# Two units of the second feed-forward product split ahead of the last Relus, a weight sum formed in SBUF, and a job stream that begins elsewhere

## The chip, the cores and the metric

The kernel runs on one core of one Trainium2 chip. The time is the device time of one execution in microseconds (us), the median of several runs. Its engines work side by side, each with its own instruction queue: TensorE (PE in the profile; PEld is its weight load), VectorE (DVE), ScalarE (ACT), GpSimd (POOL) and SyncE (SP). An instruction waits at the head of its queue until what it needs is there, and everything behind it waits too. DMAs are issued by SP and POOL here, each in its queue's order.

## The reference, cut to what matters

One layer of a streaming encoder, for 512 positions of width 1024, in float32. Three mixers (gated DeltaNet, "GDN"; stick-breaking attention; a short gated convolution) are merged by gates, projected and normed, and a feed-forward network with squared Relu follows. The part that the change is about:

```python
h2 = rms_norm(x1, norm_ffn_pre)              # x1: 512 x 1024
a = jnp.square(jax.nn.relu(h2 @ w_ff1))      # 512 x 4096
y = a @ w_ff2                                # 512 x 1024
x = x1 + rms_norm(y, norm_ffn_post)
```

## The kernel before

**Precision.** TensorE multiplies fp32r numbers. A float32 matrix is split into a rounded part `hi` and the rest `lo`, and a product is made of three: hi·hi, hi·lo, lo·hi (`mm3`, or `go` in `product`). ScalarE makes `hi` by a copy, VectorE makes `lo` by a subtraction (`split`; `wload` for weights).

**The order of the work.** The first part interleaves GDN, stick-breaking and projections by hand-written generators that `tick()` advances. `gate_branch` is the unit of the gate stage: a projection, a sigmoid into `sg`, the load of half a unit of branch weights (`wload`, 256 KB), twelve matmuls and a multiplication. It runs for branches 1 and 2 with GDN and stick-breaking work in between (the loop that makes `mp`), then for branch 0 together with the loads of the output weights `wo` (`load_wo`). The last of these makes `mg`, the merged activations, and the out-projection (`out_k`, into PSUM banks `po`) follows, with norms whose vectors `wpo` and `wff` and whose rows `x1` come over POOL's queue. Instructions are put in order by priorities; a step inside `with early():` gets a priority ahead of the place where it stands in the code, so weight loads and their splits run ahead as far as buffers allow. `g2` tiles are a shared pool of 128x512 buffers.

**First product (FF1).** 32 steps `f`, each 128 of the 4096 channels: load of 512 KB into `raw`, its split into `hl` (a ring of three), 24 matmuls, then `ff1_act`: ScalarE's Relu (L945), VectorE's squares into `aT` (L948), and for the later half the differences `X` (L951) and `W` (L953).

**Second product (FF2).** It is a two-by-two block product done with seven products in place of eight (in order Q, R, Q, R, S, V, S by the PSUM banks they go to), each of eight units `u` of 12 matmuls. Per unit, `stat` splits the left side (activations `aT`, or `X`, `W`) into `ahi` and `alo`, a ring of four, and `right` loads a 512 KB weight unit and splits it into `hl`. The first three units load into six `rw` tiles; all later ones into eight slots `ch` that share memory with FF1's input (`h2h`, `h2l`) and so come free when FF1 ends.

**The jobs.** Four of the seven products need sums or differences of weight blocks: S5, S6, S1, S7, eight tiles each in DRAM. `presum()` does one step of this stream: SP copies one block from DRAM to DRAM (the base, `dma_start` in L173), and two steps later POOL adds the other block to it by an accumulating DMA (L169). There are 32 jobs, of 512 KB each; a step is taken in FF1 for f = 3 to 27, and in the products after every fourth unit. The last product reads S7.

Of the kernel before, what the change touches and what calls it, by code (L numbers as in the profile page):

```python
# [9 lines left out]
F32 = mybir.dt.float32  # L10
F32R = mybir.dt.float32r
AF = mybir.ActivationFunctionType
ALU = mybir.AluOpType

P = 128
D = 1024
# [45 lines left out]
def trunk_kernel(ctx, tc, keys, xT, xtok, wst, wab, cst, vec, alog, dtb, wpost, wffn, wfpost, out):  # L62
# [22 lines left out]
    def mbank():  # L85
        return pp.tile([P, 512], F32, tag="mm", bufs=3, name=nm("mm"))
# [59 lines left out]
    def wsrc(n, *key):  # L146
        if key not in keys:
# [1 line left out]
        return wst[keys.index(key)][:, :n]  # L149


    S5, S6, S1, S7 = ([dp.tile([P, 1024], F32, tag=f"{n}{u}", bufs=1, name=f"{n}{u}") for u in range(8)]
                      for n in ("S5", "S6", "S1", "S7"))
    jobs = []
    for u in range(8):
        jobs.append((S5[u], ("ff2", 1, 8 + u), ("ff2", 1, u)))
# [1 line left out]
        jobs.append((S6[u], ("ff2", 0, u), ("ff2", 1, u)))  # L158
    for u in range(8):
        jobs.append((S1[u], S5[u], ("ff2", 0, u)))  # L160
    for u in range(8):
        jobs.append((S7[u], S1[u], ("ff2", 0, 8 + u)))
    added = []
    LAG = 2

    def presum():
        while added and (len(added) > LAG or not jobs):
            t, key = added.pop(0)
            nc.gpsimd.dma_start(t, wsrc(1024, *key), accum_op=ALU.add, max_dma_last_dim=4096)  # L169
        if jobs:  # L170
            t, of, plus = jobs.pop(0)
            with early():
                dep(nc.sync.dma_start(t, wsrc(1024, *of) if isinstance(of, tuple) else of), lastw[0])  # L173
            added.append((t, plus))

    def wnext(*key):
        return wload(wsrc(1024, *key))
# [624 lines left out]
    def gate_branch(dm, i, y):  # L802
        sg = g2("sg")
        ps = proj(5128 + i * D + dm * P)
        with urgent():
            act(sg, ps, AF.Sigmoid)
        w = wload(wsrc(512, "br", i, dm), 512)
        ps = mbank()
        for k in range(4):
            c = slice(k * P, k * P + P)  # L810
            mm3(ps, w[:, 0, c], w[:, 1, c], y[k][0], y[k][1], k == 0, k == 3)
            if k in (1, 3):
                tick()
        with urgent():
            nc.vector.tensor_tensor(sg, sg, ps, ALU.mult)
        return sg

    for dm in range(8):
        a = gate_branch(dm, 1, yb)
        b = gate_branch(dm, 2, yc)  # L820
        mp[dm] = g2("mp")
        nc.vector.tensor_tensor(mp[dm], a, b, ALU.add)
# [111 lines left out]

    aT = [[], []]
    X, W = [], []
    flat = lambda t: t.rearrange("p j c -> p (j c)")

    def ff1_act(f, ps):
        u = f // 2  # L940
        if f % 2 == 0:
            for i in range(2):
                aT[i].append(g2("aT", F32, (P, 2, 256)))
        r = sm.tile([P, 512], F32, tag="r", bufs=2, name=nm("r"))
        nc.scalar.activation(r, ps, AF.Relu)  # L945
        for i in range(2):
            c = slice(i * 256, i * 256 + 256)
            nc.vector.tensor_tensor(aT[i][u][:, f % 2, :], r[:, c], ps[:, c], ALU.mult)  # L948
        if f % 2 == 1 and u >= 8:
            X.append(g2("X", F32, (P, 2, 256)))  # L950
            nc.vector.tensor_tensor(flat(X[-1]), flat(aT[0][u]), flat(aT[0][u - 8]), ALU.subtract)  # L951
            W.append(aT[0][u])
            nc.vector.tensor_tensor(flat(W[-1]), flat(W[-1]), flat(aT[1][u]), ALU.subtract)  # L953
# [6 lines left out]
    for f, (w, ps) in enumerate(lead):  # L960
        ff1_mm(w, ps, slice(256, 512))
        ff1_act(f, ps)
    for f in range(3, 32):
        if f < 28:
            presum()
        w = wnext("ff1", f)
        ps = mbank()
        ff1_mm(w, ps, slice(0, 512))
        ff1_act(f, ps)

    wfp = sm.tile([P, D], F32, tag="L", bufs=1, name="wfp")
    nc.gpsimd.dma_start(wfp, wfpost.partition_broadcast(P))
    NU2 = 8
    A = {(i, k): aT[i][8 * k:8 * k + 8] for i in range(2) for k in range(2)}  # L980
    ou, x1a = {}, {}
    NJ, NR = 4, 3
    stats = [(g2("ahi", F32R, (P, 2, 256)), g2("alo", F32R, (P, 2, 256))) for _ in range(NJ)]
    raws = [[(slice(0, 512), g2("rw")), (slice(512, 1024), g2("rw"))] for _ in range(NR)]
    turn = {"s": 0, "r": 0, "w": 0}
    slot = [0]

    def ring(what, of):
        turn[what] += 1
        return of[(turn[what] - 1) % len(of)]  # L990

    def right(src):
        if turn["r"] < NR:
            raw = ring("r", raws)
        else:
            if turn["r"] == NR:
                raws.clear()
                for _ in range(2):
                    t = hp.tile([P, 4, 1024], F32, tag="h16", name=nm("ch"))
                    raws.extend([(slice(0, 1024), t[:, i, :])] for i in range(4))  # L1000
            raw = ring("r", raws)
        for c, r in raw:
            x = nc.sync.dma_start(r, src[:, c])
            dep(x, lastw[0])
            lastw[0] = x
        turn["w"] += 1
        if turn["w"] % 4:
            hl = wp.tile([P, 2, 1024], F32R, tag="hl", bufs=3, name=nm("hl"))
            hl = (hl[:, 0, :], hl[:, 1, :])
        else:  # L1010
            hl = [wp.tile([P, 1024], F32R, tag="raw", bufs=2, name=nm("hl4")) for _ in range(2)]
        for c, r in raw:
            nc.scalar.copy(hl[0][:, c], r)  # L1013
            nc.vector.tensor_tensor(hl[1][:, c], r, rf(hl[0][:, c]), ALU.subtract)  # L1014
        return hl

    def block(k, n):
        return lambda u: wsrc(1024, "ff2", n, 8 * k + u)

    def stat(t):  # L1020
        hi, lo = ring("s", stats)
        split(flat(hi), flat(lo), flat(t))
        return hi, lo

    def product(ps, left, block, first, tail=0):
        def go(tb, a, w, f, l):
            ts_ = slice(tb * P, tb * P + P)
            for j in range(2):
                c = slice(j * 512, j * 512 + 512)
                mm(ps[tb], a[0][:, j, ts_], w[0][:, c], f and j == 0, False, not first)  # L1030
                mm(ps[tb], a[0][:, j, ts_], w[1][:, c], False, False, not first)
                mm(ps[tb], a[1][:, j, ts_], w[0][:, c], False, l and j == 1, not first)

        kept = []
        for u in range(NU2):
            with early():
                a = stat(left(u))
                w = right(block(u))
            slot[0] += 1
            if slot[0] % 4 == 0:  # L1040
                presum()
            if u >= NU2 - tail:
                kept.append((a, w, u == NU2 - 1))
                continue
            for tb in range(2):
                go(tb, a, w, first and u == 0, u == NU2 - 1)
        for tb in range(2):
            for a, w, l in kept:
                go(tb, a, w, False, l)
            yield tb  # L1050
# [20 lines left out]

    d, ga = ([g2(n) for _ in range(2)] for n in ("d", "ga"))
    Q = banks2("Q")
    for tb in product(Q, lambda u: A[1, 0][u], block(0, 0), True):
        nc.scalar.copy(d[tb], Q[tb])
    R = banks2("R")
    for tb in product(R, lambda u: X[u], block(1, 1), True):
# [15 lines left out]
    for tb in product(V, lambda u: sub(A[1, 0][u], X[u], X[u]), lambda u: S6[u], True):  # L1093
        nc.vector.tensor_tensor(d[tb], V[tb], d[tb], ALU.add)
        evac(d[tb], 2 + tb, 1)
        store(2 + tb)
    for tb in product(S, lambda u: W[u], lambda u: S7[u], False, 2):
        nc.vector.tensor_tensor(ga[tb], S[tb], ga[tb], ALU.add)
        evac(ga[tb], tb, 0)
        store(tb)  # L1100
# [85 lines left out]
```

## Time and profile before

| What | us |
| --- | --- |
| median of 3 runs | 924.14 (922.2 to 926.25) |
| the profiled execution | 924.36 |
| its span | 922.6 |
| TensorE busy | 889.2 (96%) |
| VectorE busy | 602.8 (65%) |
| ScalarE busy | 440.7 (48%) |
| GpSimd busy | 119.8 (13%) |

The span is cut by the profile into 40 equal slices; a digit of 9 is 90% busy or more. TensorE, its granted clock and the DMA engines:

```profile
PE   8999999989998999999999989999999979999996
PEclk9999999999999999999999999999999999999998
DMA  9322223221211132412243475399999529996522
```

The out-projection lies in slices 24 and 25, FF1 in slices 26 to 33, FF2 in the rest. A busy TensorE is not TensorE at full speed: its matmuls take twice as long where the clock is granted at the lower of its two levels. The rows of the trace that say more stand further down.

### The profile page before, as it was taken

Reading aid. Unit: us, or ns where it says so; the run is one execution under the profiler, and the core shown is the slowest. Engines: PE = TensorE matmul, PEld = TensorE weight load, DVE = VectorE, ACT = ScalarE, POOL = GpSimd, SP = SyncE. Lnnn points to the kernel's source line nnn. Section 1 sums busy time; section 2 is a strip of 40 time slices with the busy share of each in tenths; the row PEclk is TensorE's granted clock in tenths of the full one; section 3 lists DMA queues with packets and bytes.
Section 4 is the critical chain, followed back from the end, with each engine's and each line's share of the span. In section 5 each row is a group of like instructions: output and inputs, shape, how many; then the busy total and the mean of one; then the engine's idle time right before and its main releaser. Section 6 shows DMA issues by size and latency. Waiting matters only on the chain.

```text
span 922.6 us, 11744 instructions
## 1 busy us (share of the span) xinstructions
PE 889.2 (96%) x4204; PEld 737.7 (80%) x4204; DVE 602.8 (65%) x1046; ACT 440.7 (48%) x799; POOL 119.8 (13%) x189
## 2 busy tenths in 40 slices
PE   8999999989998999999999989999999979999996
PEld 6788888777787888888888868988888868888885
DVE  4786689988878659555555436533344447878885
ACT  7456776537776832232343333322322235566561
POOL 1003331121122120200000032011111000120000
PEclk9999999999999999999999999999999999999998
DMA  9322223221211132412243475399999529996522
GB/s 319 109 71 90 72 94 99 92 80 52 83 41 54 50 121 82 132 66 78 72 157 122 174 201 189 112 282 282 285 285 285 179 86 364 339 321 227 191 97 87
DMA packets 41883, 141.17 MB, mean 153 GB/s; under 512 B 5584, under 2 KB 5584, under 8 KB 41312
## 3 DMA queue, kind: packets, MB, share of 16 engines
q1 hardware_dynamic: 34432, 115.69, 34.9%
q0 software_dynamic: 7248, 24.68, 12.7%
q8 instruction: 33, 0.54, 0.2%
q14 instruction: 26, 0.21, 0.1%
q10 hardware_dynamic: 144, 0.04, 0.0%
HBM read 135.67 MB, written 38.27 MB: 189 GB/s over the span
## 4 chain that ended last, share of the span: by engine, by line
PE 81%; DVE 10%; ACT 3%; DMA 2%; issue 2%; POOL 0%; SPq 0%; POOLq 0%; DVEq 0%; ACTq 0%
PE mm L180 52%; PE Q L180 5%; PE R L180 5%; PE S L180 4%; PE po L180 3%; PE psv L180 3%; PE V L180 2%; DVE hl L143 2%; PE p L180 2%; DMA raw<-wst 2%; DVE c L686 2%; DVE w L678 1%; DVE z L688 1%; DVE XX L508 1%; DVE XX L514 1%
## 5 line engine op out<-in xcount | busy, mean ns | idle before, releaser
L180 PE MATMUL mm<-hh,hl 128*128 128x512 f32 x928 | 306.6, 398 | 0.7 <-ACT ct L735 0.7
L143 DVE TENSOR_TENSOR hl<-raw,hl 128x1024 fp32r<-128x1024 f32 x116 | 129.8, 1119 | 144.1 <-ACT hl L142 143.8
L142 ACT CAST hl<-raw 128x1024 fp32r<-128x1024 f32 x116 | 111.8, 964 | 225.6 <-PE mm L180 173.7
L180 PEld LDWEIGHTS mm<-hh,hl 128*128 128x128 f32 x928 | 174.7, 189 | 35.7 <-ACT ct L735 1.0
L180 PE MATMUL mm<-hl,hl 128*128 128x512 f32 x464 | 181.7, 392 | 0.0
L180 PE MATMUL mm<-h2h,hl 128*128 128x512 f32 (+1 forms) x528 | 155.2, 377 | 0.3 <-ACT h2h L188 0.2
L180 PEld LDWEIGHTS mm<-h2h,hl 128*128 128x128 f32 x528 | 97.2, 188 | 19.0 <-ACT h2h L188 0.8
L180 PEld LDWEIGHTS mm<-hl,hl 128*128 128x128 f32 x464 | 87.8, 189 | 16.1
L180 PE MATMUL mm<-h2l,hl 128*128 128x512 f32 (+1 forms) x264 | 99.5, 377 | 0.1
L1014 DVE TENSOR_TENSOR hl<-ch,hl 128x1024 fp32r<-128x1024 f32 x53 | 64.7, 1223 | 6.5 <-ACT hl L1013 6.4
L169 POOL DMA_DIRECT2D S<-wst x32 | 26.2, 820 | 301.8 <-DMA S<-wst 153.7
L180 PEld LDWEIGHTS mm<-h2l,hl 128*128 128x128 f32 x264 | 49.7, 188 | 9.3 <-DVE h2l L189 0.3
L1013 ACT CAST hl<-ch 128x1024 fp32r<-128x1024 f32 x53 | 55.4, 1046 | 0.0
L180 PE MATMUL po<-wo,mg 128*128 128x512 f32 x192 | 46.9, 400 | 3.4 <-ACT mg L188 3.4
L180 PEld LDWEIGHTS po<-wo,mg 128*128 128x128 f32 x192 | 37.0, 193 | 11.8 <-ACT mg L188 3.9
L180 PE MATMUL Q<-hl,ahi 128*128 128x512 f32 x128 | 41.4, 405 | 4.6 <-ACT hl L1013 2.8
L180 PE MATMUL S<-hl,ahi 128*128 128x512 f32 x128 | 39.4, 389 | 0.0
L180 PE MATMUL R<-hl,ahi 128*128 128x512 f32 x128 | 39.4, 389 | 0.0
L188 ACT CAST ahi<-aT 128x512 fp32r<-128x512 f32 x32 | 19.7, 623 | 31.7 <-PE Q L180 15.1
L180 PEld LDWEIGHTS Q<-hl,ahi 128*128 128x128 f32 x128 | 25.2, 197 | 10.7 <-ACT hl L1013 3.2
L948 DVE TENSOR_TENSOR aT<-r,mm 128x256 f32<-128x256 f32 x62 | 23.1, 414 | 11.2 <-ACT r L945 11.2
L652 POOL TENSOR_SCALAR_AFFINE_SELECT w<-w 128x128 f32<-128x128 f32 (+1 forms) x24 | 13.7, 580 | 118.7 <-DVE w L678 99.8
(287 smaller groups left out, 1464.9 us busy)
## 6 DMA issues: line engine op xcount, KB each, us to landing
raw<-wst SPq DMA_DIRECT2D x92, 512.0 KB, 3.3
S<-wst POOLq DMA_DIRECT2D x32, 512.0 KB, 9.0
ch<-S SPq DMA_DIRECT2D x32, 512.0 KB, 3.3
raw<-wst SPq DMA_DIRECT2D x48, 256.0 KB, 3.0
ch<-wst SPq DMA_DIRECT2D x21, 512.0 KB, 8.0
S<-wst SPq DMA_DIRECT2D x16, 512.0 KB, 8.4
S<-S SPq DMA_DIRECT2D x16, 512.0 KB, 9.1
xk<-xT SPq DMA_DIRECT2D x8, 256.0 KB, 5.5
```

What stands on the lines that cost most here:

```text
L142: nc.scalar.copy(hl[:, 0, :], raw)
L143: nc.vector.tensor_tensor(hl[:, 1, :], raw, rf(hl[:, 0, :]), ALU.subtract)
L169: nc.gpsimd.dma_start(t, wsrc(1024, *key), accum_op=ALU.add, max_dma_last_dim=4096)
L180: return nc.tensor.matmul(o, l, r, start=start, stop=stop, skip_group_check=more)
L188: nc.scalar.copy(hi, src)
L508: nc.vector.tensor_tensor(tmp[:, :, :w], X[:, :, j].unsqueeze(2).to_broadcast([P, 8, w]), L[:, j, j + 1:].unsqueeze(1).to_broadcast([P, 8, ...
L514: nc.vector.tensor_tensor(X[:, :, j + 1:], X[:, :, j + 1:], tmp[:, :, :w], ALU.subtract)
L652: nc.gpsimd.affine_select(ap, ap, pattern=[[0, n], [-1, 128]], compare_op=ALU.is_ge, fill=0.0, base=-1, channel_multiplier=1)
L686: nc.vector.tensor_tensor_scan(c[:, c0:c0 + m][:, ::-1], ones[:, 0:1].to_broadcast([P, m]), back, 0.0, ALU.mult, ALU.add)
L948: nc.vector.tensor_tensor(aT[i][u][:, f % 2, :], r[:, c], ps[:, c], ALU.mult)
L1013: nc.scalar.copy(hl[0][:, c], r)
L1014: nc.vector.tensor_tensor(hl[1][:, c], r, rf(hl[0][:, c]), ALU.subtract)
```

## The change

In the order of the code:

- S7 and its eight jobs are gone; 24 jobs are left. `right` takes a second source `plus`, which POOL adds by an accumulating DMA to the SBUF slot that SP has just loaded. The last product loads S1[u] and adds block(1, 0) in this way.
- `presum()` is called in the gate loop of branches 1 and 2, at dm = 1, 3, 5, 7, and in FF1 for f = 6 to 29. It is no longer called in the products.
- The tiles and functions of FF2's sides (`stats`, `raws`, `right`, `block`, `stat`) stand ahead of the FF1 loop. The loop ends at f = 29. For f = 30 and 31 the matmuls, and one unit of Q's operands (`unit`: `stat` and `right`, under `early()`), are written ahead of `ff1_act`; `dep` keeps Relu(30) and Relu(31) behind that unit's last cast on ScalarE, and their squares behind its last subtraction on VectorE. `product` takes these two units from `ready`.

```diff
-    S5, S6, S1, S7 = ([dp.tile([P, 1024], F32, tag=f"{n}{u}", bufs=1, name=f"{n}{u}") for u in range(8)]
-                      for n in ("S5", "S6", "S1", "S7"))
+    S5, S6, S1 = ([dp.tile([P, 1024], F32, tag=f"{n}{u}", bufs=1, name=f"{n}{u}") for u in range(8)]
+                  for n in ("S5", "S6", "S1"))
...
-    for u in range(8):
-        jobs.append((S7[u], S1[u], ("ff2", 0, 8 + u)))
...
     for dm in range(8):
+        if dm % 2 == 1:
+            presum()
         a = gate_branch(dm, 1, yb)
         b = gate_branch(dm, 2, yc)
...
+    ready, after = [], [None, None]
...
-        nc.scalar.activation(r, ps, AF.Relu)
+        x = nc.scalar.activation(r, ps, AF.Relu)
+        if ready:
+            dep(x, after[0])
         for i in range(2):
             c = slice(i * 256, i * 256 + 256)
-            nc.vector.tensor_tensor(aT[i][u][:, f % 2, :], r[:, c], ps[:, c], ALU.mult)
+            x = nc.vector.tensor_tensor(aT[i][u][:, f % 2, :], r[:, c], ps[:, c], ALU.mult)
+            if ready:
+                dep(x, after[1])
...
-    for f in range(3, 32):
-        if f < 28:
-            presum()
...
-    def right(src):
+    def right(src, plus=None):
...
             x = nc.sync.dma_start(r, src[:, c])
             dep(x, lastw[0])
             lastw[0] = x
+            if plus is not None:
+                nc.gpsimd.dma_start(r, plus[:, c], accum_op=ALU.add)
...
         for c, r in raw:
-            nc.scalar.copy(hl[0][:, c], r)
-            nc.vector.tensor_tensor(hl[1][:, c], r, rf(hl[0][:, c]), ALU.subtract)
+            after[0] = nc.scalar.copy(hl[0][:, c], r)
+            after[1] = nc.vector.tensor_tensor(hl[1][:, c], r, rf(hl[0][:, c]), ALU.subtract)
...
+    def unit(left, block, u):
+        with early():
+            src = block(u)
+            return stat(left(u)), right(*src) if isinstance(src, tuple) else right(src)
+
+    A10 = lambda u: aT[1][u]
+    for f in range(3, 30):
+        if f >= 6:
+            presum()
+        w = wnext("ff1", f)
+        ps = mbank()
+        ff1_mm(w, ps, slice(0, 512))
+        ff1_act(f, ps)
+    late = [(wnext("ff1", 30), mbank())]
+    ff1_mm(*late[0], slice(0, 512))
+    late.append((wnext("ff1", 31), mbank()))
+    ready.append(unit(A10, block(0, 0), 0))
+    ff1_act(30, late[0][1])
+    ff1_mm(*late[1], slice(0, 512))
+    ready.append(unit(A10, block(0, 0), 1))
+    ff1_act(31, late[1][1])
...
         for u in range(NU2):
-            with early():
-                a = stat(left(u))
-                w = right(block(u))
-            slot[0] += 1
-            if slot[0] % 4 == 0:
-                presum()
+            a, w = ready.pop(0) if ready else unit(left, block, u)
...
-    for tb in product(S, lambda u: W[u], lambda u: S7[u], False, 2):
+    for tb in product(S, lambda u: W[u], lambda u: (S1[u], block(1, 0)(u)), False, 2):
```

**ScalarE, from the Relu of f=29 on** (`r` is a Relu's output, `ahi` the rounded activations, `hl<-rw` the cast of half a weight unit, `ch` a slot). Before:

```order
L945 ACTIVATE r_6392<-mm_6367 128x512
L945 ACTIVATE r_6431<-mm_6404 128x512
L945 ACTIVATE r_6465<-mm_6440 128x512
L188 CAST ahi_6474<-aT_5324 128x512
L188 CAST ahi_6476<-aT_5382 128x512
L188 CAST ahi_6478<-aT_5454 128x512
L1013 CAST hl_6498<-rw_6482 128x512
L1013 CAST hl_6498<-rw_6483 128x512
L188 CAST ahi_6480<-aT_5527 128x512
L1013 CAST hl_6519<-rw_6484 128x512
L1013 CAST hl_6519<-rw_6485 128x512
L1013 CAST hl_6540<-rw_6486 128x512
```

After the change, to the last Relu:

```order
L946 ACTIVATE r_6399<-mm_6374 128x512
L186 CAST ahi_5384<-aT_5321 128x512
L1000 CAST hl_6446<-rw_5392 128x512
L1000 CAST hl_6446<-rw_5393 128x512
L946 ACTIVATE r_6453<-mm_6411 128x512
L186 CAST ahi_5386<-aT_5379 128x512
L1000 CAST hl_6485<-rw_5394 128x512
L1000 CAST hl_6485<-rw_5395 128x512
L946 ACTIVATE r_6490<-mm_6441 128x512
```

and from there on:

```order
L186 CAST ahi_5388<-aT_5463 128x512
L186 CAST ahi_5384<-aT_5609 128x512
L186 CAST ahi_5390<-aT_5535 128x512
L1000 CAST hl_6533<-rw_5396 128x512
L186 CAST ahi_5386<-aT_5683 128x512
L1000 CAST hl_6533<-rw_5397 128x512
L1000 CAST hl_1170_6555<-ch_6552 128x1024
L186 CAST ahi_5388<-aT_5757 128x512
```

The activation split and the two casts of unit 0 now stand before the second of these Relus, those of unit 1 before the third. Behind the Relus come the splits of units 2, 4 and 3, and the split of unit 5 stands between the two casts of unit 2. The splits of units 4 and 5 reuse the ring tiles of units 0 and 1.

**SP, around the last loads of the gate stage** (`raw` at L139 is a projection's weight unit or a branch's, at L832 half of a unit of `wo`; `S_72` to `S_74` are the first jobs' bases, `x1d` the store of the residual). Before:

```order
L832 DMA raw_4695<-wst 128x512
L139 DMA raw_5193<-wst 128x1024
L832 DMA raw_4701<-wst 128x512
L173 DMA S_72<-wst 16x8192
L139 DMA raw_5388<-wst 128x1024
L173 DMA S_73<-wst 16x8192
L832 DMA raw_4763<-wst 128x512
L139 DMA raw_5423<-wst 128x1024
L832 DMA raw_4769<-wst 128x512
L173 DMA S_74<-wst 16x8192
L890 DMA x1d<-x_921_4841 128x512
```

After the change:

```order
L832 DMA raw_4692<-wst 128x512
L139 DMA raw_5190<-wst 128x1024
L832 DMA raw_4698<-wst 128x512
L139 DMA raw_5398<-wst 128x1024
L832 DMA raw_4760<-wst 128x512
L139 DMA raw_5432<-wst 128x1024
L832 DMA raw_4766<-wst 128x512
L890 DMA x1d<-x_921_4838 128x512
```

The three base copies are gone from this stretch; the first four bases now stand among the loads of the gate loop of branches 1 and 2, and the loads of `raw` keep their order.

**POOL, at the first stick-breaking masks of the gate loop** (`gu` is GDN's, `w` the stick-breaking tiles that the triangle mask is applied to). Before:

```order
L391 TENSOR_TENSOR gu_2636<-cs,gah 128x512
L391 TENSOR_TENSOR gu_2638<-cs,gal 128x512
L652 AFFINE_SELECT w_2711<-w_2711 128x128
L652 AFFINE_SELECT w_2712<-w_2712 128x256
L652 AFFINE_SELECT w_2713<-w_2713 128x128
```

After the change:

```order
L389 TENSOR_TENSOR gu_2628<-cs,gah 128x512
L389 TENSOR_TENSOR gu_2630<-cs,gal 128x512
L167 DMA S_72<-wst 128x1024
L650 AFFINE_SELECT w_2703<-w_2703 128x128
L650 AFFINE_SELECT w_2704<-w_2704 128x256
L650 AFFINE_SELECT w_2705<-w_2705 128x128
```

The first job's accumulate stands between the two `gu` and the masks of the next head. In the kernel before it stood behind GDN's last norms, with two more, right before `wpo`:

```order
L613 TENSOR_TENSOR f_4221<-f_4221,half 128x4
L613 TENSOR_TENSOR f_4236<-f_4236,half 128x4
L169 DMA S_72<-wst 128x1024
L169 DMA S_73<-wst 128x1024
L169 DMA S_74<-wst 128x1024
L849 DMA wpo_4829<-wpost 128x512
```

## Rows read from the trace of the kernel before

**Rows 1.** The page, part 1: busy us (share) and instructions of each engine

```profile
PE 889.2 (96%) x4204; PEld 737.7 (80%) x4204; DVE 602.8 (65%) x1046; ACT 440.7 (48%) x799; POOL 119.8 (13%) x189
```

**Rows 2.** Waits of TensorE, the whole span: who waits, for whom: us, times, longest

```profile
PE po L180 <- ACT mg L188: 3.4, 1, 3.4
PE Q L180 <- ACT hl L1013: 2.8, 1, 2.8
...
PE Q L180 <- DVE hl L1014: 1.8, 1, 1.8
PE p L180 <- DVE ct L582: 1.7, 1, 1.7
...
PE mm L180 <- ACT sg L105: 0.9, 2, 0.6
```

**Rows 3.** Windows: busy PE, PEld, DVE, ACT, POOL; granted clock, DMA share, GB/s

```profile
290.00:300.00 10.00, 7.35 (x45) 5.88 (x44) 8.38 (x17) 4.28 (x10) 3.31 (x5) 1.00 0.15 52
545.00:550.00 5.00, 1.57 (x6) 0.93 (x5) 2.67 (x4) 1.73 (x3) 3.07 (x6) 0.93 0.29 52
550.00:555.00 5.00, 5.00 (x18) 4.01 (x17) 0.66 (x2) 2.75 (x8) 2.29 (x5) 0.73 0.99 255
596.00:754.00 158.00, 158.00 (x700) 130.78 (x699) 62.32 (x102) 42.93 (x56) 17.96 (x22) 1.00 0.85 241
758.00:760.00 2.00, 0.61 (x2) 0.52 (x3) 2.00 (x5) 2.00 (x5) 0.00 (x0) 0.50 0.61 217
```

**Rows 4.** Chain of waits, 735 to 800: start, us, what

```profile
734.99 19.28 PE mm L180 x85
...
783.52 16.55 PE R L180 x73
```

**Rows 5.** Timeline of ScalarE behind the last Relu: start, us, instructions

```profile
754.83 1.64 ACT L188 CAST ahi<-aT 128x512 fp32r<-128x512 f32 x3
```

**Rows 6.** Chain of waits, 496 to 580

```profile
506.41 3.80 DMA raw<-wst
...
526.14 5.00 DMA raw<-wst
...
538.16 7.22 DMA raw<-wst
...
548.78 20.04 PE po L180 x80
```

**Rows 7.** DMA issues at 526.6, 531.6, 538.6, 546.9, 760.8, 754: KB, us to landing

```profile
S<-wst SPq DMA_DIRECT2D x1, 512.0 KB, 5.8
...
S<-wst SPq DMA_DIRECT2D x1, 512.0 KB, 5.2
...
S<-wst SPq DMA_DIRECT2D x1, 512.0 KB, 8.0
...
S<-wst POOLq DMA_DIRECT2D x1, 512.0 KB, 5.3
...
S<-wst POOLq DMA_DIRECT2D x1, 512.0 KB, 9.3
...
ch<-wst SPq DMA_DIRECT2D x1, 512.0 KB, 3.4
```

**Rows 8.** Timelines of SP and POOL: start, us, instruction [idle before <-releaser]

```profile
280.19 0.33 SPq L139 DMA_DIRECT2D raw<-wst  x1
...
285.16 0.29 POOL L652 TENSOR_SCALAR_AFFINE_SELECT w<-w 128x128 f32<-128x128 f32 x1 [10.97 <-DVE w L678]
...
601.96 0.82 POOL L169 DMA_DIRECT2D S<-wst  x1 [2.26 <-DMA S<-wst]
```

**Rows 9.** Timelines in the last product: SP, POOL, ScalarE

```profile
865.07 0.32 SPq L1003 DMA_DIRECT2D ch<-S  x1
...
895.43 0.56 POOL L854 TENSOR_TENSOR st<-st,half 128x1 f32<-128x1 f32 x1 [70.62 <-DVE st L853]
...
903.59 1.05 ACT L1013 CAST hl<-ch 128x1024 fp32r<-128x1024 f32 x1
```

More of the change, by code (lines that the diff above doesn't have):

```diff
@@ L962, in trunk_kernel @@
         ff1_act(f, ps)
-    for f in range(3, 32):
-        if f < 28:
-            presum()
[L966 to L981, printed above, removed]
     NJ, NR = 4, 3
@@ L985, in trunk_kernel @@
     turn = {"s": 0, "r": 0, "w": 0}
-    slot = [0]
     def ring(what, of):
@@ L1023, in stat @@
         return hi, lo
+    def unit(left, block, u):
[18 more added lines that the diff above has]
+    ff1_act(31, late[1][1])
+    wfp = sm.tile([P, D], F32, tag="L", bufs=1, name="wfp")
+    nc.gpsimd.dma_start(wfp, wfpost.partition_broadcast(P))
+    NU2 = 8
+    A = {(i, k): aT[i][8 * k:8 * k + 8] for i in range(2) for k in range(2)}
+    ou, x1a = {}, {}
     def product(ps, left, block, first, tail=0):
@@ L1073, in trunk_kernel @@
     Q = banks2("Q")
-    for tb in product(Q, lambda u: A[1, 0][u], block(0, 0), True):
+    for tb in product(Q, A10, block(0, 0), True):
         nc.scalar.copy(d[tb], Q[tb])
```

## The prediction

> **What bounds the kernel now.** I read the busy shares first: TensorE is busy 889.2 of 922.6 us, 96% [rows 1], so only its gaps, and the slow clock after them, can be won back. The wait table of TensorE comes next [rows 2]: of some 33 us of idle time in all, the largest single waits are 3.4 us in the out-projection (`po`), 2.8 and 1.8 us at the first weights of the second feed-forward product (`Q`), and 1.7 us in the GDN solve (`p`). Then the windows [rows 3], whose last columns give the granted clock: in the first feed-forward product TensorE runs 158.00 of 158.00 us at 1.00 (2.4 GHz), 700 matmuls, so 0.226 us each, 5.42 us for a unit `f` of 24 matmuls and 2.71 us for a unit `u` of 12. Behind the wait of 3.4 us the clock was 0.93 and then 0.73 for five us each, partly at the lower level (1.2 GHz); behind the waits at `Q` it stood at 0.50; around the wait of 1.7 us it stayed at 1.00. Last, the chain of waits, at the seam of the two products and in the out-projection, shows what released the largest of them.
>
> **Part a, the seam between the two feed-forward products.** The last Relu's product ends at 734.99 + 19.28 = 754.27, and the second product of the seven, R, begins at 783.52 [rows 4]. Q's eight units of 2.71 us would end at 754.27 + 21.7 = 776.0, so 7.5 us are lost there: 4.6 idle [rows 2], the rest at half clock [rows 3]. The cause is ScalarE's order: after the last Relu it makes three activation splits of 1.64 us together [rows 5] before it touches the first weights. In the changed order the splits of units 0 and 1 stand ahead of the Relus of f=30 and f=31. Their sources are there: weights for units 0 to 2 have SBUF tiles of their own, and their activations are long made. TensorE then has 5.4 us of work at 754.27 without anyone's help, until 759.7. What is late next is unit 2: on ScalarE the split for unit 4 stands before its casts, and waits until TensorE has done unit 0 (757.0); the split for unit 5 stands between its two casts and waits for unit 1 (759.7 less the last matmuls). Its second half, cast and subtraction included, comes some 0.4 us (0 to 1.0) late. Unit 3 is the first from the slots that FF1's activations held; its load goes out at 754 and lands in 3.4 us, 757.5, as now, and it is wanted after 762. Of the 7.5 I take 7.1 as saved (3.0 to 7.5; the low end is the rival on unit 2).
>
> **Part b, the job stream leaves the out-projection.** In the gate and out-projection stage three DRAM-to-DRAM copies on SP and their accumulates on POOL, 1 MB of traffic each, run among the loads that the path waits for. Such a load (256 KB) landed in 3.80 us when it was alone, in 5.00 beside the first copy and in 7.22 beside an accumulate and the next copy [rows 6]. The last one, 538.16 + 7.22, sets when `wo` can be split and `mg` be made, 3.4 us later, and TensorE resumes at 548.78. It had stopped 3.4 before, at 545.3. With 3.80 the load lands at 541.96, `mg` is there at 545.4, and the wait is gone. Gone with it are 5 x 0.07 + 5 x 0.27 = 1.7 us of slow clock [rows 3] and the 0.6 us wait of `mm` on `sg` [rows 2], which hangs on the load of 5.00. Together 5.7; I take 5.3, since I see no guarantee that the stretch is as quiet as at 506. The bottom is 0: the `wpo`, `wff` and `x1` loads on POOL, which until now stand behind the third accumulate in its queue, come forward to where their buffers let them and could fill the same engines.
>
> **Part c, a new wait on POOL.** The job stream starts in the gate loop of branches 1 and 2 instead, where stick-breaking and GDN work is interleaved. SP issues the first base copy right behind a weight load at 280.19 [rows 8], thus at about 280.6. The accumulate for it must wait for the copy, and in POOL's order it stands directly before the triangle masks of the next stick-breaking head, whose first ran at 285.16 [rows 8]. The nearest copies landed in 5.2, 5.8 and 8.0 us [rows 7]; the last ran beside two other transfers. With 5.2 the accumulate starts at 286.1 (0.3 for the release) and holds POOL 0.8 us, as the one in rows 8; the mask comes at 287.0, 1.8 late (2.4 with 5.8; 4.6 with 8.0; 0 if the copy is quick). Behind the masks on VectorE stands the scan of that head, and behind the scan everything else of VectorE, the `ct` among it that TensorE's `p` waits 1.7 us for already [rows 2]. That wait grows to 3.5, the size behind which the clock did fall; I add 1.2 of the 1.7 found there. Cost 3.0, bounds 0 and 6.3 (4.6 + 1.7). The next three jobs stand on POOL among the start of the later GDN groups and before two norms; what comes later by them is the power of one norm, by some 1 us, and the weight products of the gates, which TensorE has in hand there, hide it. Cost 0, and 1 if that cover were gone.
>
> The Trainium skill ("DMA: Bandwidth & Descriptors", section "Anatomy of one DMA — SWDGE (gpsimd) path") gives 2.0 us and the bytes over 436 GB/s for one DMA on that path, an estimate of 3.2 us for 512 KB. The plain load of 3.4 us agrees, the copies and the accumulates (5.3 and 9.3) [rows 7] do not; were it true for the base copy, part c would be 0 and the sum 912.0.
>
> **Part d, the rest of the stream.** Jobs go on at f=6 to 29, as dense as before, where TensorE has no wait at all [rows 3]; the copies of S7 beside the products go, where it has none either. Worth 0 both ways; the cover is the ring of split weights, three deep, which is 16 us of FF1 work (three units).
>
> **Part e, the last product.** Its slots are now filled by the base load of S1 and a POOL accumulate, eight times. Base loads go out from 865.07, the last slot is cast at 903.59 [rows 9]. The first accumulate can start near 868.5; with the worst landing (9.3) it is there at 878, and the first cast is at about 884.5, one of eight 2.71 us apart that end at 903.59. The slack is 6 us at the first. At the last: 903.59 − 9.3 − 868.5 = 25.8 us for seven more, a pace of 3.7 us, and one accumulate in FF1 followed the one before after 2.26 us of waiting and 0.8 of its own [rows 8]. Two values of `st` that POOL computes for the store come at 895.43 [rows 9], behind these. Cost 0 (0 to 14, the rival below).
>
> **The sum.** The profiled execution took 924.36 (span 922.6 and 1.76 around it), 0.2 above the median of the runs, 924.14. 924.36 − 7.1 − 5.3 + 3.0 = 915.0.
>
> **Rivals.** First: the base copy of part c lands quickly and nobody waits. For it: at 280 no accumulate is under way, and a load of the same size takes 3.4 us [rows 7]; with that the accumulate starts at 284.3 and is off POOL at 285.1, before the mask. Against it: none of the copies read took under 5.2. Time 915.0 − 3.0 = 912.0, chance 0.17. The page on DMA named above is the rule behind it.
>
> Second: the out-projection's load is slow in any case, because the loads that POOL now issues earlier stand beside it as the copies did. For it: `wpo`, `wff` and `x1` come forward into this stage. Against it: each is 256 KB at most, a quarter of a job's traffic, and most of their buffers are free some time before the load in question goes out at 538.16. Part b falls away: 920.3, chance 0.10. The Trainium skill ("DMA: Bandwidth & Descriptors", section "Issuing engines are not separate DMA queues") has DMAs of every issuing engine share the same 16 engines; the 7.22 us of rows 6 agree.
>
> Third, the splitting ahead doesn't do what it says: the wait moves to unit 2. If the casts of unit 2 come 2.5 us late instead of 0.4, then by the ratio of before (7.5 lost for 4.6 idle) 4.1 of the 7.5 come back: about 919.0, chance 0.08. Against it: ScalarE is idle most of that time. It decides as soon as the second half of unit 2 is ready after 763.
>
> Fourth, on the other side: the accumulates into SBUF cannot keep pace. It decides where one takes over 3.7 us. If they followed one another at the pace of an `f`, 5.4 us, the eighth would land at 868.5 + 7 x 5.4 + 9.3 = 915.6, 12 us after its cast is due, and with 1.7 us of slow clock the time is 928.9. For it: landings of 5.3 to 9.3 us are all above 3.7. Against it: landings overlap, and two accumulates have followed one another at 3.1 [rows 8]; where they stood farther apart, POOL waited for their base copies. Chance 0.07.
>
> **Numbers.** Forecast 915.0 with 0.55; the rivals 0.17, 0.10, 0.08, 0.07; 0.03 for what I don't see. The range, 910.9 to 920.3, runs from the first rival with 1 us of part b's and a's upper ends to the second, and leaves out the fourth and the unseen, with the tails of the others. A difference of 0.5%, 4.6 us, is about what a measurement tells from none: faster is below 919.5, slower above 928.8. Forecast, first and third rival are faster, 0.80, less 0.02 for their tails; the second is the same, with those tails and some of the fourth; the fourth and half of the unseen are slower.
>
> **What would show it.** Right for a: no wait of TensorE on the weights of Q above 0.5 us, clock 1.00 from 754, R about 21.7 to 22.5 us after FF1's end. For b: no wait of `po` on `mg` above 0.6 us, the last gate load in about 4 us. For c: a mask on POOL near 287 behind an accumulate, and a `p` wait of about 3.5 us near 294. For e: no wait of TensorE on S's weights. A wait of S on casts of the slots, a loss of clock between 885 and 910, or a VectorE queue that takes up the delay of c would make it wrong.

## The result, and the profile after

The changed kernel took 912.35 us (median of 4 runs, 909.88 to 916.19) against 923.17 for the kernel before beside it: ratio 0.988, 95% interval 0.984 to 0.992. A second set gave 913.87 against 922.81, 0.990 (0.987 to 0.992). It is faster by 9 to 11 us; forecast were 915.0 and 9.4.

The profiled execution has a span of 908.2 us, 14.4 less than before. That is more than the change did: 4.4 of it had been gained before the first instruction that the change moves, as the table below shows. The page's first part, the changed kernel (compare [rows 1]):

```profile
PE 881.7 (97%) x4204; PEld 732.9 (81%) x4204; DVE 602.5 (66%) x1046; ACT 440.4 (48%) x799; POOL 120.2 (13%) x189
```

The waits of TensorE (us in all, times, longest), to be held against [rows 2]: `po` on `mg` and both waits of Q are gone, and `p` on `ct` has grown from 1.7 to 2.9.

```profile
PE p L178 <- DVE ct L580: 2.9, 1, 2.9
PE at L699 <- POOL z L650: 2.1, 1, 2.1
...
PE psv L178 <- ACT hl L186: 1.9, 1, 1.9
...
PE mm L178 <- ACT sg L105: 1.3, 2, 0.8
```

**The seam.** The chain of waits there (start, us, what) answers to [rows 4]: FF1 ends at 746.80, R begins at 768.98, 22.18 us later; before it was 783.52 − 754.27 = 29.25. So 7.1 us are gained.

```profile
714.84 31.96 PE mm L178 x141
746.80 22.19 PE Q L178 x96
768.98 21.08 PE R L178 x93
```

ScalarE's timeline behind the last Relu answers to [rows 5]. Unit 4's split (749.33, the first of two in that line, unit 3's the second) does stand before unit 2's first cast, and unit 5's (752.05) between unit 2's two casts, each waiting for Q:

```profile
746.88 0.60 ACT L946 ACTIVATE r<-mm 128x512 f32<-128x512 f32 x1 [3.30 <-issue]
...
749.33 1.14 ACT L186 CAST ahi<-aT 128x512 fp32r<-128x512 f32 x2 [1.34 <-PE Q L178]
750.38 0.62 ACT L1000 CAST hl<-rw 128x512 fp32r<-128x512 f32 x1
752.05 0.62 ACT L186 CAST ahi<-aT 128x512 fp32r<-128x512 f32 x1 [1.05 <-PE Q L178]
752.58 0.62 ACT L1000 CAST hl<-rw 128x512 fp32r<-128x512 f32 x1
```

What is left of the loss is in unit 2, as forecast: three gaps between its matmuls' starts are 0.33 to 0.37 us in place of 0.23, so that its twelve take 3.10 us where the other units of Q take 2.72 to 2.77.

```profile
752.08 0.96 PE L178 MATMUL Q<-hl,ahi 128*128 128x512 f32 x3
```

**The out-projection.** In the chain there (compare [rows 6]) the load of 523.80 is the one that took 5.00 before; the next, that took 7.22, is in it no more, and from 530.14 on TensorE works without a gap to 561.35.

```profile
523.80 5.15 DMA raw<-wst
...
530.14 3.02 PE mm L178 x12
533.16 28.19 PE po L178 x124
```

That last load went out at 535.96 and landed, by the table of DMA issues in that stretch, in 3.5 us. ScalarE's timeline has its split, and `mg`, which is there at 542.83; TensorE's first matmul that uses it starts at 542.98, so the wait is gone by little:

```profile
539.51 0.62 ACT L186 CAST wo<-raw 128x512 fp32r<-128x512 f32 x1 [3.91 <-DMA raw<-wst]
...
542.21 0.62 ACT L186 CAST mg<-sg 128x512 fp32r<-128x512 f32 x1 [1.58 <-DVE sg L839]
```

```profile
raw<-wst SPq DMA_DIRECT2D x1, 256.0 KB, 3.5
```

**The new wait.** SP's and POOL's timelines (compare [rows 8]): base copy out at 276.23, landed in 4.5 us, accumulate at 281.05, the mask behind it at 281.67; it would have been due at 280.8 (285.16 less the 4.4 us that this execution was ahead). The mask also reads 0.63 us long, 0.29 before, so that it ends 1.2 late, and `p` waits 1.2 longer. In the windows the granted clock of 290 to 300 is 0.83, before 1.00 [rows 3].

```profile
276.23 0.61 SPq L171 DMA_DIRECT2D S<-wst  x1
...
281.05 0.94 POOL L167 DMA_DIRECT2D S<-wst  x1 [11.19 <-DMA S<-wst]
281.67 0.63 POOL L650 TENSOR_SCALAR_AFFINE_SELECT w<-w 128x128 f32<-128x128 f32 x1
```

```profile
S<-wst SPq DMA_DIRECT2D x1, 512.0 KB, 4.5
```

```profile
290.00:300.00 10.00, 9.11 (x48) 7.81 (x49) 7.20 (x18) 5.67 (x14) 3.43 (x6) 0.83 0.09 37
```

**Where the time came from.** TensorE's matmuls come in nearly the same order in all kernels here. Matched one by one, the start in the profile of before less the start in the other tells how far ahead it is; the table has the growth of that lead, in us, from stage to stage (by the times of before).

| Kernel | to 188 | 188–285 | gate loop, 285–320 | to the end of out-projection, 320–573 | FF1 and seam, 573–778 | products, 778 on |
| --- | --- | --- | --- | --- | --- | --- |
| changed | +3.4 | +1.0 | −2.1 | +5.2 | +7.1 | 0.0 |
| changed, again | +1.2 | −1.1 | −1.4 | +5.1 | +7.0 | 0.0 |
| a_only | +0.1 | +0.1 | 0.0 | +0.4 | +7.1 | 0.0 |
| b_only | +1.5 | +1.1 | 0.0 | +5.0 | −0.5 | 0.0 |
| e_only | +3.4 | +1.2 | 0.0 | −2.0 | −0.5 | 0.0 |
| c_off | −1.7 | 0.0 | 0.0 | +4.2 | +7.0 | 0.0 |
| c_off, again | −0.4 | +0.1 | 0.0 | +4.6 | +7.0 | 0.0 |
| c_dep | −0.1 | −1.3 | −3.4 | +5.4 | +7.0 | 0.0 |
| c_dep2 | +1.2 | +1.1 | 0.0 | +4.6 | +7.1 | 0.0 |
| warm | +1.8 | −1.3 | −1.7 | +5.7 | +7.1 | 0.0 |
| warm_c_off | +2.3 | +1.1 | 0.0 | +4.6 | +7.0 | 0.0 |
| warm_c_dep2 | +2.5 | −0.1 | −0.6 | +5.7 | +7.1 | 0.0 |

The first two columns lie ahead of what the changes do to TensorE. There the executions differ by up to 5 us without regard to the kernel (warm, which adds matmuls at the start, apart). The other four are the change: 10.2 and 10.7 us in the two profiles. All leads are taken against one profile of the kernel before, and that profile has its own luck: e_only leaves the out-projection's instructions alone and is 2.0 us behind it there.

### The profile page after: what moved, and what is told of

Read it like the earlier page. It is cut to its first block, busy times and chain, and to the rows that moved or that the text cites. A ratio compares the mean times of both kernels' runs of the same rounds, so it can differ in the third digit from the quotient of the medians.

```text
span 908.2 us, 11722 instructions
## 1 busy us (share of the span) xinstructions
PE 881.7 (97%) x4204; PEld 732.9 (81%) x4204; DVE 602.5 (66%) x1046; ACT 440.4 (48%) x799; POOL 120.2 (13%) x189
## 4 chain that ended last, share of the span: by engine, by line
PE 80%; DVE 10%; issue 3%; ACT 3%; DMA 1%; POOL 1%; POOLq 0%; SPq 0%; DVEq 0%; ACTq 0%
PE mm L178 50%; PE Q L178 5%; PE R L178 5%; PE S L178 4%; PE po L178 4%; PE psv L178 2%; PE V L178 2%; DVE hl L143 2%; PE p L178 2%; DVE c L684 2%; DMA raw<-wst 1%; DVE w L676 1%; DVE XX L506 1%; DVE z L686 1%; DVE XX L512 1%
## 5 line engine op out<-in xcount | busy, mean ns | idle before, releaser
L178 PE MATMUL po<-wo,mg 128*128 128x512 f32 x192 | 45.0, 390 | 0.0
L167 POOL DMA_DIRECT2D S<-wst x24 | 19.9, 830 | 160.4 <-DMA S<-wst 123.6
L105 ACT ACTIVATE w<-w 128x512 f32<-128x512 f32 (+1 forms) x48 | 28.2, 588 | 0.2
```

What stands on the lines that cost most here:

```text
L105: x = nc.scalar.activation(*a, **k)
L178: return nc.tensor.matmul(o, l, r, start=start, stop=stop, skip_group_check=more)
```

## The experiments

**a_only**: the kernel before with the code of `ready`, `late`, `unit` and the two `dep` lines, jobs and S7 untouched.

```diff
-    for f in range(3, 32):
+    for f in range(3, 30):
         if f < 28:
             presum()
...
+    late = [(wnext("ff1", 30), mbank())]
...
+    ready.append(unit(A10, block(0, 0), 0))
+    ff1_act(30, late[0][1])
```

> The kernel before with nothing but the two units of Q split ahead of the last two Relus. Theory (the steps of the two traces, laid beside one another, show 7.0 us gained at the seam): 7.0 us faster than before, 916 to 917, with no wait of TensorE on the weights of Q above 0.5 us. Rival (the gain needs the quieter DMA engines that the rest of the change brings, since in this kernel the job stream still runs beside the loads of Q): under 4 us faster, with a wait of Q on unit 2 or 3.

918.0 us against 924.28, 0.992 (0.989 to 0.995). The chain shows FF1's end at 753.58 and R at 775.79, 22.21 us, as in the changed kernel:

```profile
734.99 18.59 PE mm L180 x82
753.58 22.21 PE Q L180 x96
775.79 14.28 PE R L180 x63
```

No product waits for its weights above 0.5 us. The median's gain, 6.3, is a little less than the 7.0 expected, and 918.0 misses the 916 to 917; the trace has 7.1 at the seam. The gain does not need a quieter job stream; the rival falls.

**b_only**: the kernel before, jobs from f=6.

```diff
-        if f < 28:
+        if f >= 6:
             presum()
```

> The kernel before with the job stream begun at f=6 in place of f=3 and nothing else, so that no base copy and no accumulate stands in the out-projection; its last jobs run later in the products. Theory: 5.3 us faster, 918 to 919, the load ahead of mg lands in under 5.3 us and the po wait of 3.4 is gone. Rival (wpo, wff and x1 fill the DMA engines in place of the jobs): as before, po wait 2 to 3.4. A second rival (the jobs that are now later collide with the products' loads): gained there, lost again behind 760, R, S or V waiting for weights.

917.62 against 924.28, 0.994 (0.991 to 0.997). That is 6.7 less, a little more than expected. The wait of `po` is gone (the last load landed in 3.5 us), `wpo`, `wff` and `x1` notwithstanding; the waits of Q stay, and no later product waits:

```profile
PE Q L180 <- ACT hl L1013: 2.8, 1, 2.8
...
PE Q L180 <- DVE hl L1014: 1.8, 1, 1.8
```

So part b is the job stream leaving that stage, and it holds by itself. Both rivals fall as they were put, by the wait of `po` and by the products; the load ahead of the last one is another matter (see part b below).

**e_only**: the kernel before with S7 formed in the slots.

```diff
-    for tb in product(S, lambda u: W[u], lambda u: S7[u], False, 2):
+    for tb in product(S, lambda u: W[u], lambda u: (S1[u], block(1, 0)(u)), False, 2):
```

> The kernel before with S7 alone replaced by the accumulate into the SBUF slots; the job stream begins where it did. Theory: no difference from before, 922 to 925, no wait of S on weights, since eight accumulates follow one another every 2.3 to 5.4 us with 7 us and more in hand. Rival: the 16 transfers per unit that leave the products make room there, 1 to 3 us faster; or the accumulates delay the last slots, 2 us and more slower.

925.65 against 924.28, 1.002 (1.000 to 1.004); the time alone doesn't tell 0 from the 2 us slower of the second rival. In the products the table has 0.0: nothing won, nothing lost there. The 2.0 us lost in the out-projection come from a stage whose instructions this kernel leaves alone.

**c_off** and **c_off_again**: the changed kernel without the job steps of the gate loop (one more step at f=30 flushes the last accumulates).

```diff
     for dm in range(8):
-        if dm % 2 == 1:
-            presum()
...
     ready.append(unit(A10, block(0, 0), 0))
+    presum()
```

> The changed kernel without the four job steps in the gate loop: its 24 jobs run at f=6 to 29, the last accumulates at f=30. Theory (the first accumulate on POOL ahead of the stick-breaking masks costs 1.2 us of wait at p and 0.8 more of slow clock behind it): about 2 us faster than the changed kernel, 910 to 911, the p wait back at 1.7. Rival 1 (the four steps are needed, since the sums come too late for the fourth product): a wait of R on its weights, slower than the changed kernel. Rival 2 (part c costs nothing, the p wait differs between executions anyway): same as the changed kernel, p wait still near 2.9.

> The changed kernel without job steps in the gate loop, beside the two above. Theory: within 1 us of the kernel whose first accumulate stands behind gu, since both have POOL free where it is waited for; both near 911 to 912.5. Rival (four jobs less in the gate loop also quiet the loads there): 1 us and more faster than that one.

913.0 against 924.28, 0.988 (0.986 to 0.991), and 913.52 against 922.18, 0.989 (0.985 to 0.992): by time no better than the changed kernel. The expected 910 to 911 was not met, nor was the second expectation: 913.52 is 2.5 more than c_dep2 beside it (911.03, below), where 1 at most was expected. R waits for no weights, so the four early steps aren't needed.

In the traces the gate loop loses nothing (0.0 twice, against −2.1 and −1.4), and `p` waits as before:

```profile
PE p L178 <- DVE ct L580: 1.7, 1, 1.7
```

Two things stand against this in the profiles. Both executions began with longer waits for the first weights (−1.7 and −0.4). And the out-projection gained 4.2 and 4.6 where the changed kernel gained 5.2 and 5.1. In c_off its last load is in the chain again, with 4.12 us:

```profile
540.37 4.12 DMA raw<-wst
```

Gate loop and out-projection together are 0.4 to 1.5 us ahead of the changed kernel's, less than the 1.4 to 2.1 of the gate loop alone; of the kernels whose out-projection is free of jobs, those that lose nothing in the gate loop gain less in the out-projection (4.2 to 5.0) than those that lose there (5.1 to 5.7). Why is not shown. So the trace confirms that the accumulate lengthens the wait; that taking it away makes the kernel faster is not shown by these runs.

**after_again**: the changed kernel, unaltered.

> The changed kernel once more, unaltered, beside the next three on the same chip. Theory (its own part of the difference is 10 us, the other 4 us between the two profiles are the first weights' arrival at the start and one slow stretch near 200 us, which differ between executions of either kernel): 912 to 914, ratio 0.988 to 0.990. Rival (the 4 us at the start belong to the change): ratio 0.985, and every profile of it with a first wait of psv under 2.0 us.

913.87, 0.990 (0.987 to 0.992). Its first matmuls had the same wait as in the first profile (1.99 and 1.95 us) and yet another speed. PE's timeline, the first five of the first product, of this execution and then of the earlier one:

```profile
6.90 2.50 PE L178 MATMUL psv<-hl,xh 128*128 128x512 f32 x5 [1.99 <-ACT hl L186]
```

```profile
6.86 1.42 PE L178 MATMUL psv<-hl,xh 128*128 128x512 f32 x5 [1.95 <-ACT hl L186]
```

So the lead of 4.4 us in the first profile is not the change's, and the rival falls: here the first two columns of the table have +1.2 and −1.1. The length of the wait alone does not tell how fast these matmuls run; the expectation of warm below, written beside this one, reads it that way.

**c_dep**: the changed kernel, the first accumulate moved behind the six masks of its head (`lastmask[0]` is the last mask made). The four steps of the gate loop call `presum(9)`, which issues base copies alone, so that this dependence decides where the accumulate stands; nothing else changes place on POOL or SP.

```diff
-            nc.gpsimd.dma_start(t, wsrc(1024, *key), accum_op=ALU.add, max_dma_last_dim=4096)
+            dep(nc.gpsimd.dma_start(t, wsrc(1024, *key), accum_op=ALU.add, max_dma_last_dim=4096), lastmask[0])
...
-            presum()
+            presum(9)
```

> The changed kernel with one instruction moved: the first accumulate stands on POOL behind the six masks of its stick-breaking head in place of ahead of them; the base copies stay where they are. Theory (the waiting accumulate at the head of POOL's queue delays the masks): the p wait falls from 2.9 to 1.7, no slow clock behind it, about 2 us faster than the changed kernel. Rival (it is the base copy's traffic beside the weight loads): p wait stays near 2.9, time as the changed kernel.

913.89, 0.990 (0.988 to 0.993): no gain. The predicted step did happen, `p` on the first `ct` is back at 1.7, but a second wait grew from 0.4 to 2.4, and the gate loop loses 3.4 in place of 2.1 and 1.4 (in a profiled execution of 916.82, 2.9 above the median):

```profile
PE p L179 <- DVE ct L589: 2.4, 1, 2.4
...
PE p L179 <- DVE ct L581: 1.7, 1, 1.7
```

POOL's and VectorE's timelines at that place show what happened. A multiplication of 128x128 on VectorE began at 295.07, when POOL was in the accumulate, and ended at 297.90, when POOL's second `gu` ended (297.81). Alone the same instruction takes 0.28; beside the first `gu` in the kernel before, the changed one and c_off 0.88 or 0.89.

```profile
294.80 0.93 POOL L168 DMA_DIRECT2D S<-wst  x1
295.43 1.38 POOL L390 TENSOR_TENSOR gu<-cs,gah 128x512 fp32r<-128x512 f32 x1
296.44 1.37 POOL L390 TENSOR_TENSOR gu<-cs,gal 128x512 fp32r<-128x512 f32 x1
```

```profile
295.07 2.83 DVE L589 TENSOR_SCALAR ct<-ct,wD 128x128 f32<-128x128 f32 x1
...
299.12 0.28 DVE L589 TENSOR_SCALAR ct<-ct,wD 128x128 f32<-128x128 f32 x1
```

**c_dep2**: the same, with the accumulate behind the two `gu` (`lastgu[0]` in place of `lastmask[0]`, set where `gu` is made).

> The changed kernel with the first accumulate moved farther down POOL's queue, behind the two products gu that follow the masks. In the kernel with the accumulate right behind the masks the p wait on the scan's ct was back at 1.7, but a VectorE multiplication of 128x128 (ct times wD) took 2.83 us in place of 0.88 while POOL ran gu, which the accumulate had put 0.6 later. Theory (that collision took the gain): with the accumulate behind gu the multiplication takes 0.9, both p waits are as without jobs (1.7 and 0.4), about 2 us faster than the changed kernel, 911 to 912. Rival (the base copies' traffic is what costs): the multiplication or the p waits stay long, 913 to 914.

911.03 against 922.18, 0.987 (0.984 to 0.991), as expected. The multiplication takes 0.88, the gate loop loses nothing, though the base copies are where the changed kernel has them:

```profile
291.44 0.88 DVE L589 TENSOR_SCALAR ct<-ct,wD 128x128 f32<-128x128 f32 x1
```

That settles the wait. What lengthened it was POOL being held at the wrong instruction, not the base copies' traffic. For the slow clock behind it, it does not settle it: warm_c_dep2 below has the same two waits (1.7 and 0.4), and its gate loop still loses 0.6, with the granted clock at 0.50 in the two us behind them. The median of c_dep2 is 2.8 below the changed kernel's of the set before it and 1.3 below that of the first set, with intervals that overlap.

```profile
292.00:294.00 2.00, 1.67 (x7) 1.60 (x7) 2.00 (x4) 0.01 (x1) 1.11 (x2) 0.50 0.00 0
```

**warm**: the changed kernel, twelve matmuls on zeros at the start.

```diff
-WN = 6
+WN = 12
```

> The changed kernel with twelve in place of six matmuls on a zero tile at the very start, ahead of the first weights; they feed nothing. Theory (executions differ in how long TensorE waits for its first weights, 1.9 to 4.1 us, and when the wait is above 2.2 its matmuls run 0.43 apart in place of 0.23 for about six us more): the wait gets shorter by about 1.5 to 2.5, the slow stretch goes, median 1.5 to 3 us faster than the changed kernel and a spread of the runs under 4 us. Rival (the spread comes from elsewhere, as from the loads in the out-projection): median and spread as the changed kernel.

912.69, 0.988 (0.985 to 0.990), six runs from 910.84 to 913.18; the unaltered kernel beside it spread from 912.14 to 916.60. The wait for the first weights is 0.5, the first matmuls run at the short spacing, here and in the two kernels below. The first product does not begin earlier (7.95 against 6.86 and 6.90): the zeros' matmuls end later. The median gained 1.2, less than expected, and the intervals overlap; the spread halved, from 4.5 to 2.3 us, under the 4 expected.

```profile
1.98 5.49 PE L178 MATMUL warm<-wr 128*128 128x512 f32 x12 [1.98 <-DVE wr L243]
7.95 1.38 PE L178 MATMUL psv<-hl,xh 128*128 128x512 f32 x3 [0.48 <-ACT hl L186]
```

**warm_c_off** and **warm_c_dep2** put this on c_off and on c_dep2.

> Both: no job steps in the gate loop (24 jobs at f=6 to 29), twelve matmuls at the start. Theory (the gains add): 2 + 2 us faster than the changed kernel, 908 to 910. Rival (the out-projection, whose wait on the load has no room left, takes up what comes early): 911 and more.

> The same with twelve matmuls on zeros at the start. Theory: 1 to 1.5 us faster again, 910 to 911, and runs within 3 us of one another. Rival (the start's gain is lost in the out-projection's load): as the kernel without them.

911.84, 0.987 (0.984 to 0.989), for warm_c_off: the expected 908 to 910 was missed, and the rival's 911 and more is what came. In its trace the gate loop loses nothing, and the out-projection gains 4.6, 1.1 less than in warm, as the rival has it; the median is 0.85 below warm's. 910.69 against 922.18, 0.987 (0.984 to 0.990), for warm_c_dep2, the lowest median of all. Against c_dep2 alone it is 0.3 us, not the 1 to 1.5 expected; the runs lie within 3.1 us of one another, about as expected. The changed kernel's two medians, 912.35 and 913.87, are 0.5 to 3.2 us higher than these two, but the intervals of the ratios overlap: that either is faster than the changed kernel is not shown.

## Why the prediction was right

**Part a** was 7.1, measured 7.1 and 7.0, and 7.1 with part a alone. The 0.4 us that unit 2 was to be late are there too: its twelve matmuls take 3.10 us in place of 2.72. ScalarE's order did it, no transfer: a_only has the gain with the job stream as before. The third rival (the wait moves to unit 2) fell: the table of waits has none.

**Part b** was 5.3, measured 5.2 and 5.1, and 5.0 with part b alone. The last load took 3.5 us where 3.80 was expected, the wait of 3.4 and the slow clock of 1.7 behind it are gone. The 0.6 us wait of `mm` on `sg` is not: the load that it hangs on took 5.15 in place of 5.00, and the wait is 0.8. No job stands beside it any more, but `wff` and the first load of `x1` do. In the kernel before, these went out behind the last load (`wff` at 548.15 first); now POOL's timeline has them at 521.51 and 524.99, and by the table of DMA issues they take 3.5 and 4.6 us. A load of the same kind that went out at 504.31, when POOL had none under way, landed in 3.6:

```profile
521.51 0.54 POOL L850 DMA_DIRECT2D wff<-wffn  x1 [1.09 <-PE mm L178]
524.99 0.54 POOL L870 DMA_DIRECT2D x<-xtok  x1 [2.94 <-DVE wo L187]
```

```profile
raw<-wst SPq DMA_DIRECT2D x1, 256.0 KB, 5.2
```

```profile
raw<-wst SPq DMA_DIRECT2D x1, 256.0 KB, 3.6
```

So the second rival (other loads take the jobs' place) fell for the last load, and what it describes is seen at the load before it; no run tests this by itself. The 0.4 us taken off the 5.7 for a stretch less quiet than hoped covered it. The agreement to 0.1 is also in part luck, since it hangs on one profile of the kernel before: against e_only's out-projection, with the same instructions, part b would read 2.0 more, as a load there took 5.86 and the slow clock lasted longer.

**Part c** was 3.0, measured 2.1 and 1.4 (1.7 in the kernel with more matmuls at the start). Sign and place were right, the size was off: the copy landed in 4.5 us (by the table of DMA issues), less than any read before, so the mask began 0.9 late, not 1.8, the `p` wait was 2.9, not 3.5, and the slow clock behind it cost 0.3 to 0.8, not 1.2. In part the next stage seems to give it back (see c_off). The three jobs that follow cost nothing, as forecast: the lead is 2.3 at 320 and 2.2 at 540. The first rival's time, 912.0, is nearer to 912.35 than the forecast, but not for its reason: the copy was not quick enough to spare POOL the wait. The estimate of 3.2 us for 512 KB from the Trainium skill ("DMA: Bandwidth & Descriptors", section "Anatomy of one DMA — SWDGE (gpsimd) path") is for DMAs that GpSimd issues; for this copy, which SP issued from DRAM to DRAM, it is too low.

**Parts d and e** were 0 and measured 0.0. The slack in e was not where the prediction had it: the first slot had 10.0 us, more than the 6 named, and the last had 2.1. POOL's and ScalarE's timelines in the changed kernel: the first accumulate, at 854.47, landed in 5.5 us, and its slot's cast began at 869.96. The eight went out in 24.5 us, 3.5 apart against the 3.7 allowed; the last went out at 879.00, landed 7.9 us later by the table of DMA issues, at 886.9, and its cast began at 889.05. The slowest took 9.9, where 9.3 was taken as the worst.

```profile
854.47 0.89 POOL L992 DMA_DIRECT2D ch<-wst  x1 [99.64 <-DMA ch<-S]
...
879.00 0.85 POOL L992 DMA_DIRECT2D ch<-wst  x1 [2.96 <-DMA ch<-S]
```

```profile
869.96 1.05 ACT L1000 CAST hl<-ch 128x1024 fp32r<-128x1024 f32 x1
...
889.05 1.05 ACT L1000 CAST hl<-ch 128x1024 fp32r<-128x1024 f32 x1
```

The fourth rival (accumulates that can't keep pace) fell, by the margin at the last slot. Its time adds up to 915.0 + 12.0 + 1.7 = 928.7, not 928.9.

**The sum.** 7.1 + 5.3 − 3.0 = 9.4 stands against 10.2 and 10.7 from the traces and 10.8 and 8.9 between the medians of the two sets. Part c, taken too large, is the difference to the traces. Of the 2.65 us between 915.0 and 912.35, 1.2 are not the change's: the kernel before took 923.17 in that set, and the forecast starts from 924.36. That the profiled execution was 14.4 shorter would have misled: 4.4 of it is in the first two columns of the table.

What stays open: why the stretch from 188 to 285 is quick in some executions and slow in others. Behind the wait of `at` on POOL's mask, 2.0 to 2.1 us in all of them, the clock fell in some (19 matmuls and 0.66 granted in six us) and not in others (25 and 1.00); no experiment aimed at it.

## What to carry to other kernels

Read what stands in front of the first needed cast in each queue at a seam: two units' splits moved ahead of two Relus gave back all but 0.4 us of a gap that looked like a matter of transfers. A background DMA stream costs where a load is waited for, and an accumulate that waits at the head of GpSimd's queue holds up whatever stands behind it; choose the place by what follows, not by free bandwidth. When such a stream leaves a stage, look at what moves up in the same queue. Before a difference between two profiles is put down to a change, match the instructions one by one and subtract what differs ahead of it.

## What the hardware showed that was not expected

**VectorE held by GpSimd.** The 128x128 multiplication by a per-row value took 0.28 us alone, 0.88 when the first `gu` ran on GpSimd, and 2.83 when it met the accumulate and two `gu` in a row. It ended when GpSimd was through, not in proportion to the overlap, and the two `gu` took 1.38 and 1.37 in place of 1.05. The Trainium skill ("SBUF — State Buffer", section "Who interferes with whom") says that such VectorE instructions can take a pair of ports that VectorE shares with GpSimd, and that whichever issues first holds it for a whole instruction while the other is blocked; the trace agrees. Here the waiting instruction, which began 0.36 us before the first `gu`, outlasted both of them, so it seems to have been passed over more than once; starts and ends on GpSimd are rough in the profile.

**The start.** After nearly equal waits (1.95 and 1.99 us) the matmuls of the first product ran at 0.23 us in one execution and 0.43 in another. In 7 to 13 us 27 matmuls stand in the first of these, 18 in the second and 13 in the kernel before, and the granted clock reads 1.00 for all three; only after a wait of 4.1 us, in c_off, does the column show it, 0.53 in 8 to 15. The number of matmuls in a window told it where the clock column did not:

```profile
7.00:13.00 6.00, 5.61 (x13) 4.45 (x14) 4.96 (x8) 5.34 (x10) 0.97 (x2) 1.00 1.04 370
```

```profile
7.00:13.00 6.00, 6.00 (x27) 4.91 (x28) 4.51 (x8) 4.82 (x9) 0.55 (x2) 1.00 1.02 365
```

```profile
7.00:13.00 6.00, 6.00 (x18) 4.73 (x19) 4.00 (x7) 4.35 (x8) 0.55 (x2) 1.00 1.02 363
```

The first of these is the kernel before, the second the changed one, the third the changed one again.
